# First rows of x at the head of two queues, and identity products while TensorE waits for block 0

## The chip, the cores and the metric

One core of one Trainium2 chip. The metric is the device time of one execution in microseconds (us), the median of several runs. TensorE (PE; PEld is its weight load), VectorE (DVE), ScalarE (ACT) and GpSimd (POOL) each work through an order of their own, fixed when the program is built; SyncE (SP) issues most transfers.

## The reference

Two decoder layers over 512 tokens of width 1024, after one layer norm of the input. The part around the change is the layer norm and the first projection, whose columns hold the queries, keys and values of two attentions and the features of a token index:

```
def reference(x, p, positions, ln_in_g, ln_in_b, w_in, ...):
    x = layer_norm(x, ln_in_g, ln_in_b)
    for i in range(DEPTH):
        x = hybrid_layer(x, p[i], positions, w_in[i], ...)
    return x

def hybrid_layer(x, p_i, positions, w_in, ...):
    h = x @ w_in
    qa, ka, va, qb, kb, vb, qi, ki, wi = jnp.split(h, cuts, axis=-1)
    ...
    qi = rope(qi.reshape(B, S, IDX_HEADS, IDX_DIM), positions)
    ki = rope(layer_norm(ki, idx_k_g, idx_k_b), positions)
    ...
    oa = swa_sink_attention(qa, ka, va, ...)
    ob = dsa_sparse_attention(qb, kb, vb, qi, ki, wi, k_top)
    x = layer_norm(DN_ALPHA * x + concat(oa, ob) @ w_o, ln1_g, ln1_b)
    g, u = jnp.split(x @ w_gu, 2, axis=-1)
    ffn = (silu(g) * u) @ w_down
    return layer_norm(DN_ALPHA * x + ffn + (p_i @ w_pp) * sigmoid(x @ w_pg), ln2_g, ln2_b)
```

## The kernel before, in words

The 512 tokens are four blocks of 128 rows, `xt[0]` to `xt[3]`. A matrix product in full precision is made of three products of rounded numbers (`mm3`, lines 325 to 327): high times high, high times low, low times high. So every operand is kept as a high part and the difference to it, the low part.

Weights come from HBM into three staging buffers (`wst`), are copied to the high part by ACT (line 278), and POOL makes the low part (line 279). A staging buffer is free again, and its next transfer can be issued, when POOL's difference has read it. High and low parts lie in one of five buffers (`wsp`), which are free again when TensorE has made its last product with them. The text numbers the weight pieces in their order: w0, w1 and w2 are the index columns of the first projection (888, 888 and 592 columns wide, 296 for each of eight steps in depth), w3 to w6 the keys and values of both attentions (768 each, 384 for each of eight steps), w7 and on the queries (1024). So w3 takes the staging buffer of w0, w4 that of w1, w5 that of w2; and w5 takes the `wsp` buffer of w0.

The start goes like this. SP issues the two short rows of the input norm (gamma and beta, `gb4`), then x of block 0 in two halves, then weights, with the x of the other blocks between them; ACT's queue issues the positions and `invf`. A transfer uses one of eight semaphores in turn, and the ninth waits until the first has landed. TensorE spreads gamma and beta over all partitions (line 345). For block 0 VectorE takes the statistics (line 372), a first pass (x minus mean, times gamma, line 397) and a last pass (times the reciprocal of the deviation, plus beta, line 400); for blocks 1 to 3 ACT makes the sums in two passes over the block (a sum, line 382, and a square, line 377) and VectorE the first and the last pass. TensorE then transposes the block in two halves (line 438), ACT copies each half to the high part `fh` (line 440) and VectorE makes the low part `fl` (line 441). Then come 24 products of 296 columns with w0, w1 and w2, eight steps in depth. VectorE normalises the index key (lines 562 to 580) and rotates features by a table of cosines and sines (line 511); POOL adds the two products (line 513), makes a high part (line 516) and a low part (line 517), and TensorE transposes them (line 523). The table comes from ACT and POOL beside all this (`rotary`, lines 473 to 491; its products on ACT are at line 473).

The program gives its parts in some order, and the build then places every engine's instructions by a timeline of its own. So an edit at one place can move instructions at others.

Of the kernel before, what the change touches and what calls it, by code (L numbers as in the profile page):

```python
# [96 lines left out]
def hybrid_kernel(ctx: ExitStack, tc: tile.TileContext, x, p, positions, ln_in_g, ln_in_b, w_in,  # L97
# [15 lines left out]
    def bank(tag, bufs, dt=F32):  # L113
        return psum.tile([128, 512], dt, name="bank", tag="bank", bufs=8)
# [7 lines left out]
    def t2k(dt=F32):  # L122
        return tmp.tile([128, 512], dt, name="t2k", tag="t2k")
# [24 lines left out]
    idr = const.tile([128, 128], F32R, name="idr")  # L148

    def load_x(t):  # L150
        for c in (slice(0, 512), slice(512, D)) if t == 0 else (slice(0, D),):
            SP.dma_start(xt[t][:, c], x[0, t * 128:(t + 1) * 128, c])


    gb4 = t2k()
    for i, row in enumerate((ln_in_g, ln_in_b)):
        SP.dma_start(gb4[2 * i:2 * i + 2], bass.AP(tensor=row.tensor, offset=row.offset, ap=[[512, 2], [1, 512]]))
    load_x(0)
    A.dma_start(posi, bass.AP(tensor=positions.tensor, offset=positions.offset, ap=[[1, 128], [128, NT]]))
    A.dma_start(invf, bass.AP(tensor=inv_freq.tensor, offset=inv_freq.offset, ap=[[0, 128], [1, 48]]))  # L160
    gb = {}
# [185 lines left out]

    def tok(t):
        return slice(t * 128, (t + 1) * 128)


    def rstd_of(var, n=1, of=1):
# [195 lines left out]
    for l in range(L):  # L548
# [277 lines left out]
        def start():  # L826
            ws = take(3)
            for t in range(NT):
                if l == 0 or t == 3:
                    to_features(t)  # L830
                    yield 0.9
                if l == 0 and t == 0:
                    with tc.issue_after(last["copy"]):
                        ln_in_sums(2)
                    ln_in_sums(3)
                    for _ in table:
                        pass
                if l == 0 and t + 1 < NT:
                    ln_in(t + 1)
                done = gi_out  # L840
                if l == 0 and t + 1 < NT:
                    done = behind(last["norm"], gi_out)
                if l == 0 and t == 2:
                    with tc.issue_after(last["norm"]):
                        V.tensor_scalar(nsink, sink, -1.0, None, op0=OP.mult)
                yield from project(ws, 296, (t,), from_f, done, 3 * (t == 3))
            ws = take(4)
            for b in ALL:
                yield from project(ws, 384, b, from_f, kv_out, 4 * (b is ALL[-1]))
            for q in QS[:NSTART]:  # L850
                yield from queries(*q)
# [240 lines left out]
```

## Time and profile before

| | us |
|---|---|
| runs shown | 1270.28, 1270.34, 1269.55 |
| median | 1270.28 |
| the profiled execution, its own time | 1271.5 |
| its span | 1269.7 |
| TensorE busy in it | 1235.5 |
| VectorE / ScalarE / GpSimd busy | 794.2 / 576.4 / 702.8 |

The rows are of the one profiled execution and count from the start of its span. A row of a timeline gives the start, the time that it covers, the engine, the line, the operation, what it writes and reads, how many instructions it holds, and in brackets the idle time ahead of it and what ended that. Line numbers of before hold for all rows.

### The profile page before, as it was taken

What the parts mean: (1) busy time and instruction counts of PE and PEld (TensorE: products, weight loads), DVE (VectorE), ACT (ScalarE), POOL (GpSimd) and SP (SyncE); (2) the same over time, 40 slices, a digit from 0 to 9 for tenths busy, and PEclk for the clock granted to TensorE, in tenths of its full rate; (3) what the DMA queues carried; (4) which work ended last, traced back from release to release, by engine and by line L of the source; (5) the groups of instructions that cost most, each with busy time, mean ns of one, the idle gap of its engine ahead of it and who ended that gap; (6) DMA issues with size and microseconds to landing.
All of it is one profiled execution on the core that took longest, in us unless ns stands there. A gap on an engine that the chain in (4) does not pass through costs nothing.

```text
span 1269.7 us, 18249 instructions
## 1 busy us (share of the span) xinstructions
PE 1235.5 (97%) x6632; PEld 1071.8 (84%) x6632; DVE 794.2 (63%) x1721; ACT 576.4 (45%) x1193; POOL 702.8 (55%) x579
## 2 busy tenths in 40 slices
PE   7999999899999999999999999999999999999996
PEld 5899988888888888888898998979888888888885
DVE  7699966573636363726676998674736364545376
ACT  6478774443434343434336786733434243433320
POOL 6886531466565656563168764333747574747422
PEclk9999999999999999999998999999999999999998
DMA  5232310343242423034032313114242323221321
GB/s 175 67 99 86 101 50 19 100 133 116 68 132 75 125 76 125 17 116 138 13 89 83 105 45 117 34 43 135 84 122 77 123 84 116 89 94 47 103 83 50
DMA packets 89122, 112.77 MB, mean 89 GB/s; under 512 B 5444, under 2 KB 65860, under 8 KB 89032
## 3 DMA queue, kind: packets, MB, share of 16 engines
q1 hardware_dynamic: 88360, 111.58, 28.1%
q8 instruction: 52, 0.85, 0.3%
q14 instruction: 38, 0.31, 0.1%
q10 hardware_dynamic: 672, 0.03, 0.0%
HBM read 109.49 MB, written 2.10 MB: 88 GB/s over the span
## 4 chain that ended last, share of the span: by engine, by line
PE 93%; DVE 2%; ACT 2%; POOL 1%; issue 0%; DMA 0%; DVEq 0%; ACTq 0%; POOLq 0%
PE bank L326 28%; PE bank L325 28%; PE bank L327 28%; PE bank L693 3%; PE bank L735 2%; PE bank L729 2%; PE bank L523 1%; PE bank L654 1%; PE bank L438 1%; PE bank L752 1%; ACT fh L440 1%; DMA invf<-in_inv_freq_dram 0%; POOL slot L517 0%; ACT t2k L377 0%; POOL wsp L279 0%
## 5 line engine op out<-in xcount | busy, mean ns | idle before, releaser
L279 POOL TENSOR_TENSOR wsp<-wst,wsp 128x1024 fp32r<-128x1024 f32 (+2 forms) x148 | 353.4, 2402 | 268.1 <-ACT wsp L278 267.5
L326 PE MATMUL bank<-fl,wsp 128*128 128x512 f32 (+1 forms) x768 | 286.6, 374 | 3.3 <-DVE fl L441 3.3
L325 PE MATMUL bank<-fh,wsp 128*128 128x512 f32 (+1 forms) x768 | 285.1, 374 | 3.4 <-ACT fh L440 3.4
L327 PE MATMUL bank<-fh,wsp 128*128 128x512 f32 (+1 forms) x768 | 284.8, 373 | 0.0
L278 ACT CAST wsp<-wst 128x1024 fp32r<-128x1024 f32 (+2 forms) x148 | 151.3, 1032 | 171.6 <-PE bank L327 130.2
L326 PEld LDWEIGHTS bank<-fl,wsp 128*128 128x128 f32 x768 | 146.2, 190 | 28.4 <-DVE fl L441 3.7
L325 PEld LDWEIGHTS bank<-fh,wsp 128*128 128x128 f32 x768 | 145.0, 190 | 29.2 <-ACT fh L440 4.4
L890 DVE TENSOR_TENSOR t2k<-bank,t2k 128x512 f32<-128x512 f32 x44 | 30.4, 692 | 221.9 <-PE bank L327 221.9
L325 PE MATMUL bank<-wsp,fh 128*128 128x256 f32 (+3 forms) x512 | 166.2, 328 | 1.6 <-ACT fh L440 1.6
L327 PEld LDWEIGHTS bank<-fh,wsp 128*128 128x128 f32 x768 | 146.2, 190 | 24.9
L327 PE MATMUL bank<-wsp,fl 128*128 128x256 f32 (+3 forms) x512 | 164.3, 323 | 1.3 <-DVE fl L441 0.8
L326 PE MATMUL bank<-wsp,fh 128*128 128x256 f32 (+3 forms) x512 | 165.5, 324 | 0.0
L257 POOL TENSOR_TENSOR wsp<-slot,wsp 128x512 fp32r<-128x512 f32 x100 | 141.6, 1444 | 28.9 <-ACT wsp L256 28.9
L325 PE MATMUL bank<-wsp,slot 128*128 128x512 f32 x392 | 153.9, 393 | 0.0
L326 PE MATMUL bank<-wsp,slot 128*128 128x512 f32 x392 | 152.6, 389 | 0.0
L327 PE MATMUL bank<-wsp,slot 128*128 128x512 f32 x392 | 148.4, 389 | 0.0
L810 DVE TENSOR_TENSOR x<-bank,x 128x512 f32<-128x512 f32 x140 | 91.5, 684 | 88.5 <-PE bank L327 88.5
L922 ACT CAST slot<-t2k 128x256 fp32r<-128x256 f32 (+1 forms) x104 | 49.8, 497 | 144.2 <-DVE t2k L890 102.6
L257 POOL TENSOR_TENSOR wsp<-t2k,wsp 128x512 fp32r<-128x512 f32 x40 | 57.6, 1450 | 92.4 <-ACT wsp L256 92.4
L325 PEld LDWEIGHTS bank<-wsp,fh 128*128 128x128 f32 x512 | 98.3, 193 | 8.0 <-ACT fh L440 2.9
L327 PEld LDWEIGHTS bank<-wsp,fl 128*128 128x128 f32 x512 | 98.0, 192 | 7.1 <-DVE fl L441 1.1
L326 PEld LDWEIGHTS bank<-wsp,fh 128*128 128x128 f32 x512 | 98.7, 193 | 5.5
(168 smaller groups left out, 2162.6 us busy)
## 6 DMA issues: line engine op xcount, KB each, us to landing
wst<-in_w_gu_dram SPq DMA_DIRECT2D x88, 512.0 KB, 3.5
slot<-in_w_down_dram SPq DMA_DIRECT2D x80, 256.0 KB, 2.8
wst<-in_w_in_dram SPq DMA_DIRECT2D x16, 512.0 KB, 3.6
wst<-in_w_o_dram SPq DMA_DIRECT2D x16, 512.0 KB, 3.6
wst<-in_w_pg_dram SPq DMA_DIRECT2D x16, 512.0 KB, 4.1
wst<-in_w_in_dram SPq DMA_DIRECT2D x8, 256.0 KB, 2.8
lng<-in_ln_g_dram SPq DMA_DIRECT2D x4, 512.0 KB, 5.0
lnb<-in_ln_b_dram SPq DMA_DIRECT2D x4, 512.0 KB, 6.0
```

The costliest lines, as they stand in the source:

```text
L257: G.tensor_tensor(w[:, 1, j], src[j], w[:, 0, j], OP.subtract)
L278: A.copy(w[:, 0, :a * n], st[:, :a * n])
L279: G.tensor_tensor(w[:, 1, :a * n], st[:, :a * n], w[:, 0, :a * n], OP.subtract)
L325: PE.matmul(o, sh, mh, start=start, stop=False, skip_group_check=again)
L326: PE.matmul(o, sh, ml, start=False, stop=False, skip_group_check=again)
L327: PE.matmul(o, sl, mh, start=False, stop=stop, skip_group_check=again)
L693: PE.matmul(ps[:, o:o + nn], qT[kind, t, g][:, j * 128:(j + 1) * 128], kT[c, s][:, k0:k0 + nn], start=(s == 0), stop=(s == 1))
L729: PE.matmul(o, vt[b0 + b][:, f:f + 128], pts[b][:, u], start=b == 0 and u == 0, stop=b == nb - 1 and u == 1)
L735: PE.transpose(ps[:, j * 128:(j + 1) * 128], es[j][:, b * 128:(b + 1) * 128], idf)
L810: V.tensor_tensor(xt[t][:, c], ps, xt[t][:, c], OP.add)
L890: V.tensor_tensor(a, ps[1, f], a, OP.mult)
L922: A.copy(h[0], src)
```

## The change

The first half of block 0's x becomes the first transfer of SP's queue and the second half the first of ACT's, ahead of gamma and beta, positions and `invf`. A helper makes products of the 128 by 128 identity into a bank that nobody reads: sixteen after gamma and beta are spread, eight behind the transposes of block 0.

```diff
     def load_x(t):
-        for c in (slice(0, 512), slice(512, D)) if t == 0 else (slice(0, D),):
-            SP.dma_start(xt[t][:, c], x[0, t * 128:(t + 1) * 128, c])
+        SP.dma_start(xt[t], x[0, t * 128:(t + 1) * 128])
...
     gb4 = t2k()
+    for q, c in ((SP, slice(0, 512)), (A, slice(512, D))):
+        q.dma_start(xt[0][:, c], x[0, :128, c])
     for i, row in enumerate((ln_in_g, ln_in_b)):
         SP.dma_start(gb4[2 * i:2 * i + 2], bass.AP(tensor=row.tensor, offset=row.offset, ap=[[512, 2], [1, 512]]))
-    load_x(0)
...
+    def warm(n):
+
+        ps = bank("warm", 1)
+        for _ in range(n):
+            PE.matmul(ps[:, :128], idr, idr, start=True, stop=True)
+
+    warm(16)
...
                     to_features(t)
+                    if l == 0 and t == 0:
+                        warm(8)
                     yield 0.9
```

The build places instructions anew on every engine. In the new order lines from 350 on are 8 higher than before, those from 829 on 10.

On ACT, at the start, the order before (`wst_119`, `124`, `130`, `135` and `142` are w0 to w4; `x1_86` is block 1, `x2_87` block 2, `x3_88` block 3; the two `fh` copies are block 0's):

```order
L473 ACTIVATE t2k_189<-t2k_178 128x192 x2
L278 CAST wsp_121<-wst_119 128x888
L278 CAST wsp_127<-wst_124 128x888
L382 ACTIVATE t2k_194,lnsum1_192<-x1_86 128x1024
L278 CAST wsp_132<-wst_130 128x592
L377 ACTIVATE t2k_198,lnvar_197<-x1_86,lnm_193 128x1024
L440 CAST fh_83<-bank_210 128x4x128
L440 CAST fh_83<-bank_217 128x4x128
L382 ACTIVATE t2k_226,lnsum1_224<-x2_87 128x1024
L278 CAST wsp_139<-wst_135 128x768
L382 ACTIVATE t2k_234,lnsum1_232<-x3_88 128x1024
L278 CAST wsp_146<-wst_142 128x768
```

and now (`wst_136`, `141`, `147`, `152` and `159` are w0 to w4; `bank_227` and `bank_234` are block 0, `bank_343` block 1):

```order
L278 CAST wsp_138<-wst_136 128x888
L481 ACTIVATE t2k_206<-t2k_195 128x192 x2
L278 CAST wsp_144<-wst_141 128x888
L390 ACTIVATE t2k_211,lnsum1_209<-x1_86 128x1024
L278 CAST wsp_149<-wst_147 128x592
L385 ACTIVATE t2k_215,lnvar_214<-x1_86,lnm_210 128x1024
L278 CAST wsp_156<-wst_152 128x768
L278 CAST wsp_163<-wst_159 128x768
L448 CAST fh_83<-bank_227 128x4x128
L448 CAST fh_83<-bank_234 128x4x128
L390 ACTIVATE t2k_252,lnsum1_250<-x2_87 128x1024
L448 CAST fh_83<-bank_343 128x4x128
```

The copy of w0 stands ahead of the rotary products, and the copies of w3 and w4 ahead of block 0's `fh`.

On POOL, in the stretch that ends with the features of block 3, the order before (`t2k_479` and `slot_477` are of block 2, `t2k_551` and `slot_549`, `slot_580` of block 3; `wst_149`, `152` and `155` are w5 to w7):

```order
L513 TENSOR_TENSOR t2k_479<-t2k_479 128x4x32
L279 TENSOR_TENSOR wsp_513<-wst_149,wsp_513 128x768
L516 CAST slot_477<-t2k_479 128x8x32
L279 TENSOR_TENSOR wsp_527<-wst_152,wsp_527 128x768
L279 TENSOR_TENSOR wsp_538<-wst_155,wsp_538 128x1024
L513 TENSOR_TENSOR t2k_551<-t2k_551 128x4x32
L517 TENSOR_TENSOR slot_477<-t2k_479,slot_477 128x8x32
L516 CAST slot_549<-t2k_551 128x8x32
L517 TENSOR_TENSOR slot_549<-t2k_551,slot_549 128x8x32
L517 TENSOR_TENSOR slot_580<-t2k_581,slot_580 128x2x64
```

and now (`t2k_505` and `slot_503` are of block 2, `t2k_577` and `slot_575`, `slot_606` of block 3; `wst_166`, `169` and `172` are w5 to w7):

```order
L521 TENSOR_TENSOR t2k_505<-t2k_505 128x4x32
L524 CAST slot_503<-t2k_505 128x8x32
L525 TENSOR_TENSOR slot_503<-t2k_505,slot_503 128x8x32
L279 TENSOR_TENSOR wsp_539<-wst_166,wsp_539 128x768
L279 TENSOR_TENSOR wsp_553<-wst_169,wsp_553 128x768
L279 TENSOR_TENSOR wsp_564<-wst_172,wsp_564 128x1024
L521 TENSOR_TENSOR t2k_577<-t2k_577 128x4x32
L524 CAST slot_575<-t2k_577 128x8x32
L525 TENSOR_TENSOR slot_575<-t2k_577,slot_575 128x8x32
L525 TENSOR_TENSOR slot_606<-t2k_607,slot_606 128x2x64
```

Block 2's differences stand ahead of w5, and w5 to w7 stand together.

On VectorE, between block 1 and block 3 in the new order (`bank_343` and `bank_350` are block 1 transposed):

```order
L405 SCALAR_TENSOR_TENSOR x2_87<-x2_87,lnm_251,bank_110 128x512
L365 TENSOR_SCALAR lnv1_359<-lnvar_255 128x1
L366 TENSOR_SCALAR lns1_360<-lnv1_359 128x1
L449 TENSOR_TENSOR fl_84<-bank_343,fh_83 128x4x128
L371 TENSOR_SCALAR lnt1_361<-lns1_360,lnv1_359 128x1
L449 TENSOR_TENSOR fl_84<-bank_350,fh_83 128x4x128
L570 BN_STATS kst6_339<-bank_312 128x6
L372 TENSOR_SCALAR lns1_360<-lnt1_361,lns1_360 128x1
L405 SCALAR_TENSOR_TENSOR x3_88<-x3_88,lnm_259,bank_108 128x512
```

Both low parts of block 1 stand ahead of the rest of block 2's deviation; before, block 3's first passes and block 2's steps stood ahead of them.

## Rows read from the trace of the kernel before

**Rows 1.** Table of stretches: span, busy time (instructions) of each engine, granted clock, transfers

```profile
56.00:200.00 144.00, 143.88 (x1054) 136.25 (x1053) 123.98 (x372) 106.60 (x302) 86.74 (x111) 1.00 0.27 81
```

**Rows 2.** Timeline of TensorE at the end of its last early wait

```profile
51.30 1.43 PE L523 MATMUL bank<-idr,slot 128*128 128x128 f32 x10 [2.54 <-POOL slot L517]
```

**Rows 3.** Timeline of ACT around block 0's copies

```profile
8.72 1.63 ACT L473 ACTIVATE t2k<-t2k 128x192 f32<-128x192 f32 x6 [5.69 <-POOL t2k L463]
10.25 1.75 ACT L278 CAST wsp<-wst 128x888 fp32r<-128x888 f32 x2
...
14.91 1.05 ACT L440 CAST fh<-bank 128x512 fp32r<-128x512 f32 x2
15.85 1.06 ACT L382 ACTIVATE t2k<-x 128x1024 bf16<-128x1024 f32 x1
...
17.15 0.82 ACT L278 CAST wsp<-wst 128x768 fp32r<-128x768 f32 x1
```

**Rows 4.** Issues on SP; then issues by tile: count, KB, us to landing

```profile
1.43 0.83 SPq L152 DMA_DIRECT2D x<-in_x_dram  x2
2.31 0.96 SPq L240 DMA_DIRECT2D wst<-in_w_in_dram  x2
...
x<-in_x_dram SPq DMA_DIRECT2D x1, 256.0 KB, 6.0
wst<-in_w_in_dram SPq DMA_DIRECT2D x1, 444.0 KB, 6.9
x<-in_x_dram SPq DMA_DIRECT2D x1, 512.0 KB, 8.3
wst<-in_w_gu_dram SPq DMA_DIRECT2D x88, 512.0 KB, 3.5
```

**Rows 5.** Timeline of POOL at the start

```profile
6.78 0.51 POOL L458 TENSOR_TENSOR t2k<-posf,invf 128x192 f32<-128x192 f32 x1 [3.64 <-DMA invf<-in_inv_freq_dram]
...
7.82 0.87 POOL L463 TENSOR_SCALAR t2k<-t2k 128x192 f32<-128x192 f32 x1
...
11.72 2.08 POOL L279 TENSOR_TENSOR wsp<-wst,wsp 128x888 fp32r<-128x888 f32 x1
13.74 0.60 POOL L477 TENSOR_TENSOR t2k<-t2k 128x192 f32<-128x192 f32 x1
```

**Rows 6.** Timeline of VectorE: low parts, block 2's last pass, block 2's rotation

```profile
16.43 1.28 DVE L441 TENSOR_TENSOR fl<-bank,fh 128x512 fp32r<-128x512 f32 x2
...
26.76 1.40 DVE L400 SCALAR_TENSOR_TENSOR x<-x,lns,bank 128x512 f32<-128x512 f32 x2
...
37.58 0.74 DVE L511 TENSOR_TENSOR t2k<-bank,tab 128x256 f32<-128x256 f32 x2
```

**Rows 7.** Table of stretches, columns as in rows 1: VectorE is the third

```profile
24.00:32.00 8.00, 7.08 (x49) 6.25 (x49) 8.00 (x31) 5.22 (x14) 4.00 (x10) 1.00 0.24 69
```

**Rows 8.** Timeline of POOL in its last early run

```profile
38.08 0.88 POOL L513 TENSOR_TENSOR t2k<-t2k 128x128 f32<-128x128 f32 x2 [0.76 <-DVE t2k L511]
38.91 1.85 POOL L279 TENSOR_TENSOR wsp<-wst,wsp 128x768 fp32r<-128x768 f32 x1
...
41.41 4.20 POOL L279 TENSOR_TENSOR wsp<-wst,wsp 128x768 fp32r<-128x768 f32 x2
...
48.51 0.97 POOL L516 CAST slot<-t2k 128x256 fp32r<-128x256 f32 x3
49.44 1.80 POOL L517 TENSOR_TENSOR slot<-t2k,slot 128x256 fp32r<-128x256 f32 x3
```

**Rows 9.** Timeline of TensorE: block 0's transposes, block 1's first product

```profile
13.28 1.97 PE L438 MATMUL bank<-idf,x 128*128 128x128 f32 x8 [3.12 <-DVE x L400]
...
23.79 0.40 PE L325 MATMUL bank<-wsp,fh 128*128 128x296 f32 x1 [0.65 <-ACT fh L440]
```

**Rows 10.** Table of stretches, columns as in rows 1: TensorE is the first

```profile
17.16:20.50 3.34, 3.34 (x13) 3.34 (x14) 2.94 (x9) 3.34 (x7) 3.26 (x4) 1.00 0.70 186
...
24.90:27.50 2.60, 2.60 (x19) 2.60 (x20) 2.60 (x12) 1.57 (x5) 1.96 (x6) 1.00 0.57 188
```

## The prediction

> **What bounds the kernel now.** I read the table of stretches first. From 56 to 200 us TensorE is busy for 143.88 of 144.00 us [rows 1]: there only its own work counts, and a delay ahead of it passes through to the end. So the question is when TensorE gets past its last wait before 56 us. The timeline of TensorE names it: the ten transposes at L523 begin at 51.30, after 2.54 us of waiting for POOL's difference at L517 [rows 2]. The timeline of POOL shows work without a gap from 38.08 to there: sums of rotated features, three differences of weights (L279), copies and differences of index features [rows 8]. What the change does to the time is therefore what it does to the end of this run, 51.24 (49.44 + 1.80) [rows 8]. The profiled execution took 1271.5 us, 1.2 above the median of 1270.28; I work out a shift against its rows and add it to the median. A measurement of this kernel can tell about 0.2% from no change, 2.5 us.
>
> **The diff alone costs next to nothing.** The transfers of x's first rows are issued from 1.43 on [rows 4], behind two small ones; now they head SP's queue and ACT's, at about 0.7. The 24 identity products stand where TensorE waits anyway: the gap ahead of the first transposes is 3.12 us [rows 9]. A 128-column product costs 0.14 us by the ten of [rows 2] (1.43 / 10), so sixteen cost 2.3 us and eight 1.1, inside waits. What counts is that the build places other instructions anew. ACT's order has the two 768-column weight copies (w3, w4) ahead of the copies fh of block 0; before, they stood behind the sums of blocks 2 and 3. POOL's order has the weight differences w5 to w7 behind all of block 2's features; before, the first stood ahead of them.
>
> **When fh of block 0 comes.** Before, ACT makes it at 14.91 [rows 3]. Now w4 has to be copied first. It goes into the staging buffer that w1 leaves, so its transfer waits for POOL's difference of w1. ACT begins with w0, then come the six rotary products, then w1.
> - w0 landed 6.9 us after its issue at 2.31, at 9.2 [rows 4]. The queue now starts 0.7 earlier with the same bytes ahead; I take 8.6. The ends: 9.2 as before, and 7.1 if x flows much sooner. With 0.87 for the copy (half of the pair in [rows 3]) ACT is done with w0 at E = 9.5.
> - The rotary products also need invf, which POOL takes up at 6.78, and two more POOL instructions, the last ending at 8.69 [rows 5]. The transfer of invf now stands behind half of x on ACT's queue: at one end 8.7 again, at the other, if it is taken up at 8.3, some 1.5 later, 10.2. So E lies between 8.0 (7.1 + 0.87) and 10.2; I keep 9.5, nearest to the landing of w0.
> - Six products 1.53 (8.72 to 10.25) and w1 0.87: E + 2.4 [rows 3]. POOL meanwhile: difference of w0 2.08, one rotary sum 0.60 [rows 5], so E + 2.7; difference of w1 2.08: E + 4.8. From the end of such a difference (11.72 + 2.08 = 13.80) to the copy of what its buffer takes next (17.15) it was 3.35; the copy 0.82 [rows 3, 5]. Sum: fh at s = E + 8.9 = **18.4 against 14.91, 3.5 us late**; early end 16.9.
> - On SP the transfer of block 1's x stands eight places behind x's first half and now waits for it to land, near 7 (0.7 + 6.0 [rows 4]); w2 and the x of blocks 2 and 3 are queued behind it. It took 8.3 us in the crowd, and transfers of its size take 3.5 later in the kernel [rows 4]: it lands at 10.5 or 15. I take 10.5, since w0 and w1 are out of the way by then; at 15 its sum, w2, square, w3 and w4 on ACT end at s = 19.8, the late end.
>
> On the two queues the Trainium skill has a rule (DMA: Bandwidth & Descriptors, Issuing engines are not separate DMA queues): transfers issued by several engines run on the same 16 DMA engines, and only time of issue is saved. If instead the second queue brought bandwidth of its own, w0 would come at the early end and the sum below would be 1.5 us lower. The trace of before cannot decide it, since all of x is on one queue there.
>
> **What of this is caught up.** While fh waits, the passes over block 1 go on, so block 1 is normalised when block 0's copies come. From s ACT has two copies (1.05), a sum, a square and a sum pass (1.06 each by [rows 3], and 0.4 for the mean and the reads): fh of block 1 at s + 4.6 = 23.0. Before, TensorE took up block 1 at 23.79, after a wait for the same copy [rows 9]. The 3.5 us are gone there.
>
> They come back in part, because VectorE's order has both low parts (fl) of block 1 ahead of the work on blocks 2 and 3. From the first of them, at s + 5.15, to the rotation of block 2's features VectorE works without a gap: four low parts 2.6 (1.28 a pair), four last passes 2.8 (1.40 a pair), two first passes 1.4 (as long), three rotations 1.1 (0.74 a pair) [rows 6], and 43 short ones. In the stretch 24 to 32 VectorE does 31 instructions in 8.00 us [rows 7]; without its ten long ones, some 6.0 us, that is 0.10 each, and since some now wait for one another I take 0.14: 6.0. Together 13.9, then block 2's rotation, 0.74: s + 19.8, begun at 37.5; before, it began at 37.58 [rows 6]. On the way block 2's last pass comes at 28.1, against 26.76 [rows 6].
>
> **The end of POOL's run.** After that: sums 0.9, three copies 1.0, three differences 1.8 [rows 8], and 0.5 in which POOL is still at block 1's features: s + 24.0 = 42.4 for the difference of w5, against 38.91. By then TensorE has to free w5's buffer, with the first third of block 3's products: block 3's last pass ends at s + 15.5, then come its transposes, 24 products of 384 columns and that third, to s + 22.5 at the full clock, s + 24.0 at half for part of it; ACT's copy of w5 adds 0.8. A cold clock thus costs up to 0.9; I take half, 0.45. From w5 on: weight differences 1.85 + 4.20, four sums 1.65 (0.88 a pair, two shorter), copies 0.97, differences 1.80 [rows 8], 10.5 in all. POOL ends at 18.4 + 24.0 + 0.45 + 10.5 = 53.35, **2.1 us after 51.24**. TensorE is the bound behind it and its work is the same, so this is the shift: 1270.3 + 2.1 = **1272.4**. Own range: s moves it by -1.5 and +1.4, the clock by 0.45 either way, the short instructions by up to -0.7, where block 3 becomes the bound; with these partly together 0.2 to 3.5 us, 1270.5 to 1273.8.
>
> **Rivals.** *TensorE late for w5.* The clock column reads 1.00 in both stretches, but 13 products took 3.34 us at first, 0.26 each, and later 19 took 2.60, 0.14 each [rows 10]: the levels of 1.2 and 2.4 GHz. If block 2 is met at the lower one, its first fourteen products cost 1.6 us more and the wider ones behind them up to as much: the third ends at s + 25.5, w5 starts at s + 26.3 instead of s + 24.45, 1.9 later: 1274.3. For it: block 2's transposes come 1.3 us later while block 1 ends as before, so TensorE waits there for longer than before. Against it: the wait of 0.65 us at 23.79 [rows 9] left the rate up. It decides from the point at which the third ends after s + 23.2. Slower.
>
> *The intent holds.* Some fifteen products of block 0 ran 0.12 us slower than later ones [rows 10]; warm from the start they would save 1.8 us, and x may be there 1 us sooner: 2.8, 1267.5. For that, ACT's two copies would have to be done before x is ready, with w4 landed near 12 instead of 17.6; the steps above leave no way there unless transfers run far faster than they did. Faster.
>
> *Nothing reaches the end.* If w0 lands at 7.1, s is 16.9, and with VectorE's short instructions at 0.10 and a warm clock POOL ends within 0.6 us of before: 1270.3. For it: POOL's work is the same in kind and number, only its order differs. No change.
>
> **How the numbers follow.** Forecast, a late fh mostly caught up: 0.50, of which 0.10 is above 2.5 us. TensorE late: 0.25. Nothing: 0.15. The intent: 0.10. Slower by over 0.2%: 0.10 + 0.25 = 0.35; within: 0.40 + 0.15 = 0.55; faster: 0.10. The range leaves out the intent and the far side of the late clock: 1269.5 to 1275.0, that is 0.8 below no change and 0.7 above the late clock, for small moves of order that the build makes up to 250 us.
>
> **What would show it.** Right: the copy of w4 stands just ahead of fh of block 0 on ACT, and fh comes near 18.4; block 1's products start near 23.5; block 2's transposes near 29; POOL takes w5 near 43, and TensorE's last early wait ends near 53.4; from there on every interval is as before. Wrong: fh of block 0 before 16, TensorE past that wait at or before 51.3, or a wait after 56 us that before had not.

## The result, and the profile of the changed kernel

| | us |
|---|---|
| before, median of 4 runs | 1270.31 (1269.55 to 1270.72) |
| changed, median of 4 runs | 1276.86 (1274.68 to 1278.76) |
| ratio | 1.0052, 95% interval 1.0031 to 1.0072 |
| profiled execution of before: span, own time | 1269.7, 1271.5 |
| profiled execution of the change: span, own time | 1276.7, 1278.76 |

The change costs 6.55 us. The sign is the forecast's, the size is three times its 2.1 us, and 1276.86 lies outside the range of 1269.5 to 1275.0. Of the four executions two took 1274.68 and 1275.37 us at a mean granted clock of 0.990 and two 1278.35 and 1278.76 at 0.988; the profiled one is the slowest.

The table of stretches of the changed kernel, columns as in [rows 1]:

```profile
160.00:200.00 40.00, 38.68 (x238) 33.93 (x237) 25.81 (x74) 26.10 (x68) 13.56 (x14) 1.00 0.17 53
56.00:200.00 144.00, 142.50 (x1014) 134.25 (x1014) 118.63 (x364) 104.60 (x299) 85.93 (x113) 0.98 0.26 78
```

Against [rows 1], where TensorE was busy for 143.88 of 144.00 us at a clock of 1.00, it is now busy for 142.50 at 0.98, and nearly all of what it lost lies between 160 and 200 us. The timeline of TensorE gives three places: the end of the last early wait [rows 2], a later wait, and the transposes of blocks 0 and 1 behind the next layer norm, which serve as a mark, since from there both kernels run alike (busy 56.65 us of the 60 from 200 to 260, and 380.00 of the 380 from 260 to 640, in both).

```profile
55.24 1.51 PE L531 MATMUL bank<-idr,slot 128*128 128x128 f32 x10 [4.94 <-POOL slot L525]
173.89 0.44 PE L760 MATMUL bank<-idf,rb 128*128 128x128 f32 x2 [1.32 <-POOL rb L717]
233.55 1.91 PE L446 MATMUL bank<-idf,x 128*128 128x128 f32 x16
```

The mark in the kernel before:

```profile
226.87 1.91 PE L438 MATMUL bank<-idf,x 128*128 128x128 f32 x16
```

The last early wait ends 3.94 us later (55.24 against 51.30 [rows 2]). The mark comes 6.68 us later. In between lies the new wait of 1.32 us for POOL's copy L717. The rest, 6.68 - 3.94 - 1.32 = 1.42 us, is put down here to the granted clock. The table of stretches for TensorE alone (span, busy time, clock, transfers) of the change, behind its wait:

```profile
54.00:56.00 2.00, 0.76 (x6) 0.59 0.00 0
56.00:58.00 2.00, 2.00 (x11) 0.50 0.00 0
58.00:60.00 2.00, 2.00 (x8) 0.50 0.00 0
60.00:62.00 2.00, 2.00 (x10) 0.70 0.00 0
```

and of before, behind its own:

```profile
50.00:52.00 2.00, 0.70 (x6) 0.88 0.00 0
52.00:54.00 2.00, 2.00 (x11) 0.50 0.03 8
54.00:56.00 2.00, 2.00 (x11) 0.77 0.00 0
```

Half clock (1.2 in place of 2.4 GHz) follows the wait in both kernels. In the change TensorE works under it from its return at 55.24 to about 61.2, 6.0 us; before from about 51.5 to 54.9, 3.4 us. At half speed that is (6.0 - 3.4) / 2 = 1.3 us more, near the 1.42 us that are left.

**Where the lateness of 3.94 us arises.** The timeline of ACT around block 0's copies, which answers to [rows 3]:

```profile
15.29 0.83 ACT L278 CAST wsp<-wst 128x768 fp32r<-128x768 f32 x1 [0.66 <-DMA wst<-in_w_in_dram]
17.11 0.83 ACT L278 CAST wsp<-wst 128x768 fp32r<-128x768 f32 x1 [0.98 <-DMA wst<-in_w_in_dram]
17.85 1.07 ACT L448 CAST fh<-bank 128x512 fp32r<-128x512 f32 x2
```

and of TensorE at the start, which answers to [rows 9]:

```profile
4.87 7.16 PE L345 MATMUL bank<-t2k,idf 4*128 4x512 f32 x8 [4.87 <-DMA t2k<-in_ln_in_b_dram]
11.96 3.67 PE L355 MATMUL bank<-idr 128*128 128x128 f32 x16
15.43 1.93 PE L446 MATMUL bank<-idf,x 128*128 128x128 f32 x8
17.01 1.95 PE L355 MATMUL bank<-idr 128*128 128x128 f32 x8
```

fh of block 0 waits for w3 and w4 until 17.85. x came early (VectorE's statistics begin at 4.43 instead of 7.41), but gamma and beta, now behind it, came late: their spreading begins at 4.87 instead of 3.00 and takes 7.16 us. VectorE's last pass over block 0 waits for it twice, 0.96 us each, and ends at 12.81. Then the sixteen products stand in the way until 15.63: each takes 0.23 us, not 0.14. (This is the pace that such products have at a granted clock of 0.50, 0.22 us in e11 below, though the clock column reads 1.00 for the first 30 us.)

The timelines of POOL and of VectorE between 42 and 56 us show the other end, which answers to [rows 8]:

```profile
39.21 1.85 POOL L525 TENSOR_TENSOR slot<-t2k,slot 128x128 fp32r<-128x128 f32 x3
42.97 6.01 POOL L279 TENSOR_TENSOR wsp<-wst,wsp 128x768 fp32r<-128x768 f32 x3 [1.91 <-ACT wsp L278]
48.94 0.88 POOL L521 TENSOR_TENSOR t2k<-t2k 128x128 f32<-128x128 f32 x2
51.70 0.79 POOL L521 TENSOR_TENSOR t2k<-t2k 128x64 f32<-128x64 f32 x2 [1.88 <-DVE t2k L519]
52.44 0.98 POOL L524 CAST slot<-t2k 128x256 fp32r<-128x256 f32 x3
53.38 1.81 POOL L525 TENSOR_TENSOR slot<-t2k,slot 128x256 fp32r<-128x256 f32 x3
```

```profile
44.10 0.20 DVE L570 BATCH_NORM_STATS2 kst<-bank 128x6 f32<-128x32 f32 x1 [5.84 <-PE bank L327]
45.45 1.20 DVE L365 TENSOR_SCALAR lnv<-kmv 128x2 f32<-128x2 f32 x1
46.69 2.32 DVE L366 TENSOR_SCALAR lns<-lnv 128x2 int32<-128x2 int32 x1
51.33 0.29 DVE L519 TENSOR_TENSOR t2k<-kin,tab 128x128 f32<-128x128 f32 x1
```

w5 starts at 42.97 and the three differences end at 48.98. Then POOL runs out of work for 1.88 us and waits for the rotated key of block 3, whose norm VectorE could not begin before 44.10. Before, that norm began at 39.90 and its rotation at 46.10, while POOL still had differences to make: no wait.

w5 was held up as well. POOL had finished block 2's features at 41.06 (39.21 + 1.85) and then waited 1.91 us for ACT's copy of w5, and this copy waited for TensorE to free the buffer of w0. The timeline of ACT, and the table of stretches for TensorE while it works on block 2:

```profile
42.06 0.84 ACT L278 CAST wsp<-wst 128x768 fp32r<-128x768 f32 x1 [5.28 <-PE bank L327]
```

```profile
30.00:32.00 2.00, 1.62 (x7) 0.62 0.00 0
32.00:34.00 2.00, 2.00 (x11) 0.53 0.00 0
```

Fourteen products of block 2 took 0.25 us each from 30.44 to 33.80, in place of 0.14: 1.5 us more. e15 (see below) has the change's orders up to here, and its clock is 1.00 at block 2. In its timeline of POOL w5 starts 2.1 us sooner and the run ends at 53.12 instead of 55.19:

```profile
40.88 6.02 POOL L279 TENSOR_TENSOR wsp<-wst,wsp 128x768 fp32r<-128x768 f32 x3 [0.42 <-ACT wsp L278]
51.31 1.81 POOL L526 TENSOR_TENSOR slot<-t2k,slot 128x256 fp32r<-128x256 f32 x3
```

In e6, which has these orders too, it ends at 53.08. So about 2 us of the 3.94 are not in every execution of the same orders: 1.5 are block 2 at the lower level, and fh of block 0 came 0.6 us sooner there (17.29 in e15, 17.28 in e6).

### The profile page after: what moved, and what is told of

The parts are those of the page before. It is cut to its first block, busy times and chain, and to the rows that moved or that the text cites. A ratio compares the mean times of both kernels' runs of the same rounds, so it can differ in the third digit from the quotient of the medians.

```text
span 1276.7 us, 18298 instructions
## 1 busy us (share of the span) xinstructions
PE 1241.1 (97%) x6656; PEld 1077.5 (84%) x6656; DVE 793.5 (62%) x1721; ACT 577.1 (45%) x1193; POOL 702.6 (55%) x579
## 3 DMA queue, kind: packets, MB, share of 16 engines
q1 hardware_dynamic: 88216, 111.31, 28.1%
## 4 chain that ended last, share of the span: by engine, by line
PE 89%; DVE 4%; ACT 2%; issue 2%; POOL 2%; DMA 1%; SPq 0%; DVEq 0%; POOLq 0%; ACTq 0%
PE bank L325 27%; PE bank L326 27%; PE bank L327 27%; PE bank L701 2%; PE bank L743 2%; PE bank L737 2%; POOL wsp L279 1%; PE bank L531 1%; DMA wst<-in_w_in_dram 1%; DMA wst<-in_w_pg_dram 1%; PE bank L662 1%; PE bank L446 1%; PE bank L760 1%; ACT fh L448 0%; DVE lnt L371 0%
```

## The experiments

Three theories stood against each other at first. **O**: the order that the build makes on ACT and POOL sets the time. **T** and **P**: the transfers, or the products, cost it by themselves. **C**, on the granted clock, came with the trace of the change. The kernel before was run beside each (medians 1270.97 to 1271.28). Executions of one kernel differ by up to 6 us here, and the reason is part of the findings. "Wait ends" is when TensorE takes up block 3's ten transposes, "mark" is as above, both of the profiled execution.

| | median us (range) | ratio to before, interval | wait ends | mark |
|---|---|---|---|---|
| e1 first rows only | 1274.98 (1273.92 to 1276.26) | 1.0023 to 1.0047 | 51.15 | 228.83 |
| e9 first rows, eight | 1274.94 (1270.93 to 1275.65) | 1.0016 to 1.0033 | 50.20 | 227.43 |
| e2 first rows, sixteen | 1278.24 (1273.48 to 1278.76) | 1.0040 to 1.0069 | 54.00 | 231.92 |
| e5 products only | 1274.63 (1270.47 to 1276.16) | 1.0022 to 1.0046 | 52.79 | 228.44 |
| e3 change, copies held back | 1272.61 (1270.36 to 1275.46) | 1.0007 to 1.0027 | 52.63 | 228.25 |
| e7 change, L717 ahead | 1275.48 (1273.90 to 1276.17) | 1.0024 to 1.0051 | 54.89 | 231.74 |
| e4 before, 16 in the wait | 1270.04 (1266.56 to 1271.91) | 0.9982 to 1.0000 | 50.74 | 224.94 |
| e6 change, 32 in the wait, late | 1278.44 (1276.35 to 1281.23) | 1.0047 to 1.0077 | 54.89 | 232.81 |
| e15 change, 36 in the wait, in time | 1274.80 (1273.41 to 1275.37) | 1.0020 to 1.0041 | 53.17 | 230.42 |
| e8 before, waits filled | 1267.39 (1265.75 to 1269.51) | 0.9967 to 0.9986 | 51.78 | 225.94 |
| e10 the same, filled more | 1264.71 (1263.81 to 1265.35) | 0.9935 to 0.9961 | 51.39 | 225.55 |
| e12 first rows, filled | 1267.62 (1265.07 to 1270.83) | 0.9964 to 0.9983 | 54.84 | 231.04 |
| e11 x behind gamma, filled | 1269.83 (1265.99 to 1270.36) | 0.9977 to 0.9994 | 53.95 | 229.95 |
| e13 first rows, all waits filled | 1264.91 (1264.33 to 1267.54) | 0.9945 to 0.9973 | 51.75 | 225.89 |
| e14 x behind gamma, all waits filled | 1264.84 (1264.40 to 1265.45) | 0.9943 to 0.9970 | 51.15 | 225.24 |

**Which part.** e1 is the change without products:

```diff
-    warm(16)
...
-                    if l == 0 and t == 0:
-                        warm(8)
```

> The change without any identity product: only x's first rows lead the two queues. In the build's order ACT has block 0's copies fh ahead of the copies of w3 and w4 again, as before. Theory O (the order of ACT and POOL that the build makes sets the time): fh of block 0 at 13 to 15 us, TensorE past its last early wait at 50 to 52 us, time 1268.5 to 1271.5, no more than 1.5 us above before. Rival T (the transfers themselves cost the time: positions, invf, gamma and beta now stand behind x): the last early wait still ends at 54 us or later, time 1274 to 1278.

Its timeline of TensorE:

```profile
47.06 0.54 PE L529 MATMUL bank<-idr,slot 128*128 128x128 f32 x4 [0.42 <-POOL slot L523]
49.12 0.75 PE L529 MATMUL bank<-idr,slot 128*128 128x128 f32 x4 [1.52 <-POOL slot L523]
51.15 1.51 PE L529 MATMUL bank<-idr,slot 128*128 128x128 f32 x10 [0.72 <-POOL slot L523]
169.21 0.44 PE L758 MATMUL bank<-idf,rb 128*128 128x128 f32 x2 [1.32 <-POOL rb L715]
```

The place was O's, 51.15, even 0.15 us ahead of before, and the time was T's, 1274.98. So the two theories had left something out. The wait of [rows 2] is cut into pieces here (0.42, 1.52 and 0.72 us), the clock falls at the end of the second (0.50 from 49 us on), and the wait of 1.32 us near 170 is the change's.

e9 keeps the eight products, e2 the sixteen:

```diff
-    warm(16)
```

> The change without the sixteen products ahead of block 0's transposes; the eight stay. In the build's order ACT has block 0's copies fh ahead of w3 and w4, as without any products; POOL's copy L717 stands behind the weight difference, as in the change. Theory S (the sixteen are what puts fh late: they run at half clock, 3.67 us, and end at 15.6 us when block 0's x is ready near 12.9 us, and the build answers them with w3 and w4 ahead of fh): fh of block 0 at 14 to 15 us, the last early wait ends at 51 to 52.5 us, time 1274 to 1276, as with the first rows alone. Rival O (any products bring the late order): last early wait ends at 54 us or later, time 1276.5 or more.

```diff
-                    if l == 0 and t == 0:
-                        warm(8)
```

> The change without the eight products behind block 0's transposes; the sixteen stay. In the build's order w3 and w4 stand ahead of fh of block 0 on ACT, as in the change. Theory O: fh of block 0 near 17.9 us, the last early wait ends at 54 to 55.5 us, time 1274.5 to 1278.5, as in the change. Rival P (the products' own work on TensorE costs the time, above all the eight, which stand between block 0's transposes and its first products): a third of it is gone, the last early wait ends 1 to 2 us sooner than 55.24 us, time 1273 to 1275.

e9 behaves like e1 (fh of block 0 at 13.69, time 1274.94), e2 like the change (fh at 17.81, wait ends at 54.00): with the sixteen the build puts w3 and w4 ahead of fh, with the eight it does not. e9's wait ended even sooner than expected, at 50.20.

e5 has the products alone, with the transfers as before:

```diff
+    warm(16)
...
+                    if l == 0 and t == 0:
+                        warm(8)
```

> The 24 identity products alone, transfers as before. In the build's order the copy of w3 stands between the two copies fh of block 0 on ACT and w4 behind them, and the copy L717 stands ahead of the weight difference that it follows in the change. Theory O (order of ACT and POOL sets the time): half the lateness at most, the last early wait ends at 51 to 53.5 us, no wait of over 0.7 us for L717 before 200 us, time 0 to 3 us above before. Rival P (the products' own work costs the time): the last early wait ends at 54 us or later, time 5 to 7 us above before.

The wait ends at 52.79, as O had it, 1.5 us late; block 1's products ran at half clock in this execution (0.50 from 26 to 28 us), so not all of it need be the products' own work. The median is 3.7 us above the kernel before beside it, over what O allowed, though the profiled execution took only 1270.47: such a spread is the clock's, see below. Each part alone costs 3.7 us, both together 6.6.

**The two orders undone.** e3 holds the copies of w3 and w4 behind fh in the whole change:

```diff
-            A.copy(w[:, 0, :a * n], st[:, :a * n])
+            with tc.issue_after(last["copy"]) if i in (3, 4) else nullcontext():
+                A.copy(w[:, 0, :a * n], st[:, :a * n])
```

(with the weights of these two taken up only after block 0's transposes: two places fewer at first in the budget `room`.)

> The whole change, all 24 products and the transfers, but the copies of w3 and w4 on ACT are held behind the copies fh of block 0. Theory O: fh of block 0 at 13 to 15.5 us, the last early wait ends at 50 to 52 us, no wait of TensorE for L717 of over 0.5 us between 100 and 200 us, time 1268.5 to 1271.5. Rivals T and P (transfers or products cost the time by themselves): the last early wait ends at 54 us or later, time 1274 to 1278.

1.3 us above the kernel before beside it in place of 6.6: the order is the larger part. The wait for L717 is gone as well. But fh came at 16.98, not by 15.5, and the wait's end (52.63) and the time (1272.61) lie above O's ranges too. Its timelines of TensorE and ACT say why:

```profile
12.40 3.68 PE L356 MATMUL bank<-idr 128*128 128x128 f32 x16
16.98 0.59 ACT L449 CAST fh<-bank 128x512 fp32r<-128x512 f32 x1 [2.01 <-PE bank L447]
```

The sixteen products hold TensorE until 16.08, and block 0's transposes wait behind them. Two things limit what e3 says. With the copies held back the build also puts POOL's order back: one weight difference stands ahead of block 2's, as before. In every run the two orders go together, so none shows which of them costs the time. And the two traces differ by more than the order: the change's wait ended at 55.24 and e3's at 52.63, 2.6 us sooner, but e15's, with the change's orders and block 2 at full clock, ended at 53.17, only 0.5 us later than e3's.

e7 changes only POOL's order near 170 us, in the whole change (`rbs` lists the copies L717 as they are made):

```diff
-            G.tensor_tensor(w[:, 1, :a * n], st[:, :a * n], w[:, 0, :a * n], OP.subtract)
+            with tc.issue_after(rbs[-2]) if i == 21 else nullcontext():
+                G.tensor_tensor(w[:, 1, :a * n], st[:, :a * n], w[:, 0, :a * n], OP.subtract)
```

> The whole change, with one weight difference on POOL (1024 columns, 2.39 us) held behind the copy L717 that it now delays. Nothing ahead of 160 us moves. Theory O: the wait of TensorE of 1.32 us at 173.89 is gone, at most 0.65 us as in before's second layer, and the first transposes of the next norm come at 232.2 us instead of 233.55; time about 1.3 us below the change. Rival: the wait goes elsewhere (the weights come late in place of the copy), a new wait of about 1 us stands between 170 and 230 us, transposes at 233 us or later.

The wait at 173.89 is gone, no other stands in its place, and the median is 4.5 us above the kernel before beside it in place of 6.6, 2.1 less where 1.3 were expected; the two intervals overlap, so it is the row that shows the gain and not the time. This is the third piece of the 6.68 us, and it arises 120 us behind the change: the build, starting from other times, placed a difference of 2.39 us ahead of a copy of 0.40 us that TensorE waits for.

**The clock.** e4 takes the kernel before and fills its last early wait:

```diff
             def turns():
+                if l == 0 and t == 3:
+                    warm(16)
```

> The kernel before, with sixteen identity products on TensorE in its last early wait, just ahead of the ten transposes of block 3's features. Theory C (the granted clock is lost in that wait of 2.54 us and the 3.45 us behind it run at 0.52, so each such wait costs its length and 1.4 to 1.7 us more): the products fill the wait, the transposes and the 384-column products behind them run at full clock (0.17 us each instead of 0.32), the time is 1.2 to 1.7 us below before: 1268.6 to 1269.1. Rival N (the clock falls whatever stands there, or products of the identity do not hold it): the 384-column products still take 0.32 us to 54.8 us, time within 0.5 us of before.

The clock is 1.00 from 50 to 62 us, the transposes take 1.04 us in place of 1.43, and the mark comes 1.93 us sooner. Of this 0.56 is the earlier end of the wait and 1.37 is left for the clock, within C's 1.2 to 1.7. The median fell by 1.24 us, at the edge of what can be told (interval up to 1.0000): what is won here is partly lost behind the next waits, where in the profiled execution the clock then stayed low for nearly 7 us from 229.9, against 3.4 us before.

e8 fills those too, in both layers:

```diff
+                if t == 3:
+                    warm(16 if l == 0 else 24)
...
             if first:
                 to_features(0)
                 to_features(1)
+                warm(20)
```

> The kernel before, with identity products in all waits of TensorE behind which its granted clock falls: 16 in the last early wait, 24 in the same place of the second layer (wait of 3.85 us), 20 ahead of the first products of the feed-forward part in each layer (waits of 1.47 and 1.64 us). Theory C: the four stretches at half clock (of before's rows about 1.7, 1.7, 2.5 and 1.3 us lost) go, the time is 5 to 7 us below before, 1264 to 1266.5, and executions lie closer together than those of before. Rival N: products stand in the way, or the clock falls behind all the same: no more than 2 us below before.

3.6 us below before, less than expected. Of the four stretches one was left, in the second layer:

```profile
663.87 2.90 PE L356 MATMUL bank<-idr 128*128 128x128 f32 x24
667.83 1.51 PE L530 MATMUL bank<-idr,slot 128*128 128x128 f32 x10 [1.06 <-POOL slot L524]
```

The products end 1.06 us before POOL is ready, and from 668 to 671 the clock is 0.50. e10 has 20 products in the first place, 32 in the second and 28 ahead of the feed-forward part:

```diff
-                    warm(16 if l == 0 else 24)
+                    warm(20 if l == 0 else 32)
...
-                warm(20)
+                warm(28)
```

> The kernel before with the waits filled, but 20, 32 and 28 products in place of 16, 24 and 20. Theory C (the clock is lost when an idle time is left in these places): the stretch at 0.50 from 668 to 672 us, which was left with 24 products and a rest of 1.06 us of waiting, goes; time 1 to 2 us below the first filling (1267.39), 1265.4 to 1266.5. Rival N: the added products outlast the waits and cost as much, time 1267 to 1268.5.

1264.71 us, 6.3 below the kernel before beside it, and below even C's range. The clock is 1.00 in every stretch of 4 us until the last product near 1252, and the five executions lie within 1.6 us. That also explains the spread of the others. Each execution has a mean granted clock on record, and the time goes with it: of the 82 executions of the kernel before beside these runs, the fifteen at 0.993 took 1268.6 us on average, the 54 at 0.991 1271.1 and the ten at 0.990 1272.0. The spread is the length of the stretches at half clock, and where there are none it goes.

The same reading says how the change's loss divides. At a clock of 0.990 the kernel before took 1272.0 us, the change 1274.68 and 1275.37, and e3 1274.27 and 1274.72. So at the same clock e3 gains about 0.5 us on the change, and the rounding of the clock alone is worth as much (by before's executions 0.001 goes with some 1.2 us). Most of what e3 gave back goes with the clock. The likely reason is its shorter wait (3.00 us in place of 4.94), but no run shows that.

In the change itself, e6 puts 32 products ahead of the ten transposes:

```diff
             def turns():
+                if l == 0 and t == 3:
+                    warm(32)
```

> The whole change, and 32 more identity products in its last early wait. In the build's order the copy L717 comes ahead of the weight difference again. Theory C (the granted clock after the wait is a cost of its own): the 6.2 us at half clock behind the wait go, which gives back 3.1 us; with the later wait of 1.3 us gone too, the first transposes of the next norm come 4.0 to 4.6 us earlier than 233.55, at 229 to 229.6, and the time is 2 to 3 us above before (the lateness of 3.9 us of the first wait less the 1.7 us that before itself loses at half clock). Rival N: the products do not hold the clock, or stand in the way: first transposes at 232 us or later, time 5 us or more above before.

A miss, and N's second case. The timelines of TensorE and of POOL:

```profile
50.27 4.82 PE L355 MATMUL bank<-idr 128*128 128x128 f32 x32 [2.08 <-DVE work L667]
54.89 1.48 PE L531 MATMUL bank<-idr,slot 128*128 128x128 f32 x10
```

```profile
51.24 1.84 POOL L525 TENSOR_TENSOR slot<-t2k,slot 128x256 fp32r<-128x256 f32 x3
```

The products waited 2.08 us for a bank that VectorE was still reading. The clock fell at about 52.8 although TensorE worked from 50.27 on, and the products, slowed by it, ended at 55.09, though POOL had been done at 53.08: they held the transposes up by 1.8 us. So e6 did not try C, which needs products that fill the wait and no more. e15 holds a bank for them from block 2 on:

```diff
+                if l == 0 and t == 2:
+                    last["bank"] = bank("warm", 1)
+                    warm(2, last["bank"])
...
+                if l == 0 and t == 3:
+                    warm(34, last["bank"])
```

> The whole change with 36 more products in its last early wait, in a bank that is held for them, so that they begin when TensorE runs out of work; POOL's copy L717 ahead of the weight difference, as where they came too late. Theory C: granted clock 1.00 from 46 to 62 us, the first transposes of the next norm at 228.6 to 229.8 us in place of 232.81 where they came too late, time 1273 to 1275.5, 3 us below that (1278.44). Rival L (the lateness of the point is all): transposes at 231.5 us or later, time 1277 or more.

The median is 1274.80, 3.6 us below e6 (3.6 above the kernel before beside it, where e6 was 7.5 above) and in C's range. The mark, 230.42, is 0.6 us later than C's range, since 0.94 us of waiting was left and a shorter stretch at half clock stayed (0.50 from 54 to 56, 0.90 from 56 to 58), and 1.1 us of shorter waits between 140 and 180 us. It comes 2.39 us sooner than in e6; 1.72 of this is the earlier start of the transposes (53.17 against 54.89), so e15 leaves 0.7 us for the clock. The firmer evidence for C is e4, e10 and e13.

**The transfers without the waits.** e12 is e1 with e10's products:

```diff
+                if t == 3:
+                    warm(20 if l == 0 else 32)
...
+                warm(28)
```

> The transfers of the change (x ahead of gamma and beta) without its 24 products, and with the waits filled (20, 32, 28). In the build's order POOL's copy L717 stands ahead of the weight difference again. Theory R (of the 3.7 us that the first rows alone cost, 1.3 is the wait for L717 and the rest the clock behind scattered waits): both are gone, time within 1 us of the filling alone, 1265 to 1267.5. Rival T (the transfers cost time by themselves): 2 to 4 us above the filling alone.

e11 is e10 with gamma and beta first on SP's queue, then x's first half, and its second half first on ACT's:

```diff
-    load_x(0)
+    for q, c in ((SP, slice(0, 512)), (A, slice(512, D))):
+        q.dma_start(xt[0][:, c], x[0, :128, c])
```

> The kernel with the waits filled (20, 32, 28), and x's second half as the first transfer of ACT's queue, while gamma and beta stay first on SP's queue ahead of x's first half; no products at the start. Theory G (in the change the early x is held up by gamma and beta, which now land behind it and whose spreading over the partitions takes TensorE 7.16 us): the spreading starts at 3.0 to 3.5 us again, x's statistics at 5 to 6.5 us, block 0's transposes at 10.7 to 11.5 us in place of 13.28; the last early wait ends 0.5 to 1.5 us sooner, time 0 to 1.5 us below the filling alone. Rival L (the start is caught up before 50 us, or is not what bounds it): last early wait within 0.5 us of the filling alone, time the same within 1 us.

Both came out 3 to 5 us above e10: e12 as T had it, e11 above what either G or L allowed. The timeline of TensorE of e11:

```profile
48.68 0.75 PE L530 MATMUL bank<-idr,slot 128*128 128x128 f32 x4 [1.52 <-POOL slot L524]
49.79 4.36 PE L356 MATMUL bank<-idr 128*128 128x128 f32 x20
53.95 1.47 PE L530 MATMUL bank<-idr,slot 128*128 128x128 f32 x10
```

But the products stood in the wrong place: with these transfers the wait lies ahead of block 2's second group of transposes, the clock falls there, and the 20 products, at 0.22 us each, hold block 3's transposes until 53.95, 3.3 us after POOL was ready (50.66). e13 (on e12) and e14 (on e11) split them:

```diff
-                    warm(20 if l == 0 else 32)
+                    warm(9 if l == 0 else 32)
...
                     qiT[t, j] = slot()
+                    if l == 0 and t == 2 and j == 1:
+                        warm(11)
```

> As with the first rows and the waits filled, but 11 products go between the two groups of four transposes of block 2's features (the wait of 1.52 us) and 9 ahead of the ten of block 3. Theory C (only the clock behind the scattered waits made that kernel 3 us slower than the filling alone): granted clock 1.00 from 46 to 60 us, TensorE past block 3's wait at 51.5 to 52.5 us in place of 53.95 to 54.84, time 1263.5 to 1266, within 1.2 us of the filling alone (1264.71). Rival T (the transfers cost time by themselves): 1267 or more.

> The same filling with gamma and beta first on SP's queue and x's second half on ACT's. POOL's run ended at 50.66 us there, 0.5 to 0.6 us sooner than before and than the filling alone. Theory G: TensorE past block 3's wait at 50.6 to 51.2 us, time 0 to 1 us below the filling alone, 1263.7 to 1264.9. Rival: the wait stands elsewhere and nothing is left of the gain, 1265 to 1266.

The three rows of the split in e13:

```profile
48.03 1.42 PE L355 MATMUL bank<-idr 128*128 128x128 f32 x11
50.40 1.11 PE L355 MATMUL bank<-idr 128*128 128x128 f32 x9
51.75 1.05 PE L529 MATMUL bank<-idr,slot 128*128 128x128 f32 x10 [0.24 <-POOL slot L523]
```

1264.91 and 1264.84, each 6.3 us below the kernel before beside it, as e10. So T falls: the transfers cost nothing by themselves that can be measured. e14 lies within G's ranges (the wait ends at 51.15, against 51.39 in e10), but the 0.13 us by which its median is below e10's cannot be told from nothing: G is neither shown nor refuted, and what x's early arrival brings is too small to measure. In e11 the start shows where it goes, in the timelines of TensorE and ACT:

```profile
10.81 2.03 PE L445 MATMUL bank<-idf,x 128*128 128x128 f32 x8
14.65 0.61 PE L325 MATMUL bank<-wsp,fh 128*128 128x296 f32 x1 [1.81 <-ACT fh L447]
```

```profile
12.08 0.67 ACT L278 CAST wsp<-wst 128x592 fp32r<-128x592 f32 x1
14.03 1.05 ACT L447 CAST fh<-bank 128x512 fp32r<-128x512 f32 x2
```

The transposes come 2.5 us sooner than in [rows 9], but ACT still has the copies of w0 to w2, the rotary products and block 1's sums ahead of fh, which comes 0.9 us sooner than in [rows 3].

## Why the prediction was wrong

**Right.** The bound and the place [rows 1, 2]: TensorE from 56 us on, released by POOL's run. The order: w3 and w4 ahead of fh, fh at 17.85 (18.4 predicted), block 1's second copy at 22.98 (23.0), block 2's last pass at 27.38 (28.1), its rotation at 36.32 (37.5). The order is the cause of the larger part: e2, with the sixteen and the late order, is 7.0 us above the kernel before beside it and e9, without them, 3.9; e7, with the late order, 4.5 and e3 1.3. Whether it is ACT's order or POOL's, which goes with it, no run shows.

**Right by luck.** w5 at 42.97 (42.85 in the sum). POOL was free for it at 41.06, not at 42.4, and TensorE, on block 2 at the lower level, held it back by 1.91 us. Without that, in e6 and e15, w5 starts at 40.9 and POOL's run ends at 53.1, near the 53.35 of the sum, because w5 is 2.0 us sooner than in the sum and the work behind it 1.7 us longer.

**The step that failed first** is "From w5 on: weight differences 1.85 + 4.20, four sums 1.65, copies 0.97, differences 1.80, 10.5 in all". It took 12.2 us (42.97 to 53.38 + 1.81), and as long in e2, e6, e7 and e15, which have the same order. The sum followed POOL alone. I had worked out for w5 that TensorE makes 24 products of 384 columns ahead of block 3's own and left the same delay out for block 3's key: its norm on VectorE began at 44.10 instead of 39.90, took 7.2 us to the rotation, and POOL waited 1.88 us. With the 2.1 us forecast that makes the 3.94 but for 0.04, yet only because block 2's lower level had put w5 where the sum had it.

Part of these 7.2 us is in two instructions on two elements per row, L365 and L366: 1.20 and 2.32 us, the second against a median of 0.15 for its line. L366 ends at 49.01 and POOL's three differences at 48.98. In before the same instruction took 1.79 us, also under a difference. The Trainium skill (SBUF — State Buffer, SBUF: two separate sides) says that VectorE in some modes and GpSimd share a pair of ports, which one instruction holds to its end; the times of the rows agree with that. They don't show that L365 and L366 use that pair, and no experiment tried it.

**The second step** is "TensorE is the bound behind it and its work is the same, so this is the shift". Its work was the same, but the clock and the order were not: about 1.4 us for the longer stretch at half clock (e4 gave back as much by filling before's wait), 1.3 us for L717 (e7). I had said that a wait after 56 us that before had not would show the forecast wrong, and had priced none.

**A third, smaller one** is "sixteen cost 2.3 us and eight 1.1, inside waits". They took 3.67 and 1.95 us, 0.23 and 0.24 each, and the sixteen ended 2.8 us after x was ready. In the change this hid behind w4; where w4 no longer stands ahead of fh, the wait ends 1.3 us (e3) and 1.5 us (e5) later than in before, with the stretch at half clock in e5 as a part of it.

**The rivals.** "TensorE late for w5" came nearest in time, 1274.3, and in the profiled execution its step occurred: block 2 met the lower rate (clock 0.62 from 30 to 32 us, 0.53 from 32 to 34), and ACT's copy of w5 began at 42.06, 24.2 us after fh and thus past the s + 23.2 from which the prediction lets TensorE decide. Its fourteen products cost 1.5 us more (1.6 forecast), the wider ones behind them nothing. w5 still came before its 44.7, since fh and POOL were sooner than in the sum. In e6 and e15 it did not occur. "The intent holds" failed as said, on ACT's order, and e14 shows that even a better start would have brought nothing that can be measured. The range held only what can move one point; e1, whose point was 0.15 us early and whose time was 3.7 us up, shows that the point alone does not carry the time.

On the rule that several issuing engines use the same 16 DMA engines (the Trainium skill, DMA: Bandwidth & Descriptors, Issuing engines are not separate DMA queues), the transfer rates in 40 slices of the first 20 us, of before and of the change, have the same top, 441 and 439 GB/s. The two queues brought x forward and took gamma and beta back; w0's copy began at 8.26 (at 7.50 to 8.69 in the other runs with x on both queues), nearer the 8.6 taken than the 7.1 that more bandwidth would have given.

```profile
GB/s 0 0 0 9 11 5 10 102 96 174 268 272 365 394 395 397 424 402 390 421 407 441 402 417 389 259 181 119 70 45 109 335 296 18 12 82 356 313 89 104
```

```profile
GB/s 0 0 0 61 90 238 397 256 66 141 226 287 333 377 374 393 334 378 423 418 405 416 439 367 226 166 267 324 171 60 82 329 331 53 84 315 322 49 0 0
```

## What to carry to other kernels

Price a wait of TensorE as its length plus the half clock behind it, and fill it with products that nobody reads: ahead of the first piece of the wait, in a bank that is free by then, ending just before the release. A single trace of a late point can hold a stretch at half clock ahead of it that other executions lack: read the clock there too, and compare traces of the same order. Where a build places every engine's order anew, follow each chain that meets at the point, not only the one that was last before, and look for swaps far behind the edit. Bringing an input forward is worth what the next engine's order lets through, here 0.9 of 2.5 us at the first copy and nothing that can be measured at the end.

## What the runs showed of the hardware

- The granted clock fell to half behind waits of 2.54 us (before), 1.52 us with work on both sides (e1), 1.06 (e8) and 0.94 (e15). It did not fall behind a rest of 1.16 us ahead of the feed-forward part (e8, 231.49). Behind waits of 1.10 and 0.38 us at block 2 it fell in the change, behind 1.14 and 0.38 us at the same place it stayed 1.00 in e15. So the length alone does not decide.
- It can fall after TensorE is back at work: at about 52.8 in e6, 2.5 us after its return.
- It then stayed low for about 3.4 us (before, from 51.5 and from 232.4) or nearly 7 (e4, from 229.9; before, from 669.3), and at the same place, ahead of the feed-forward part, it was 3.4 us in before and e3 and nearly 7 in e1, e2 and e6. Five executions of the kernel without such stretches lie within 1.6 us (e10) and six within 1.1 (e14); of e13's seven, one took 1267.54 at a mean clock of 0.994, the others at most 1265.57 at 0.997 or 0.998. Those of before spread over 1267.60 to 1273.03.
- At the start the 296-column products took 0.25 us each and then 0.14, while the granted clock read 1.00 for both. The pace changed at 20.5 us in before, and with the change's orders near 20.3 in the change and 23.1 in e7, where w5 came 1.8 us later than in e15 although block 2 was at full clock in both.
- Two-element instructions of VectorE (L365, L366) took up to 2.32 us while POOL made weight differences, and the longest ended with them (49.01 against 48.98 us, in the change).
